# A two-layer decoder trunk on one core: the second layer's retention values as one seven-product block multiplication, its weight sums made during the first layer's MLP

## The chip, the cores and the metric

The kernel runs on one core of a Trainium2 chip. A core has a matrix engine (TensorE, PE in the profile; its weight loads have their own row, PEld), a vector engine (VectorE, DVE), a scalar engine (ScalarE, ACT), GpSimd (POOL), and SyncE (SP), which here issues nearly all DMAs, in order, from one queue. The metric is the device time of one execution in microseconds (us). A matmul multiplies a stationary block of 128x128 by a moving block 128 deep and up to 512 wide and adds into a bank of PSUM (128 partitions by 512 floats; there are eight banks).

## The reference: what is computed

There are 512 tokens, a model width of 1024, and two layers. Each layer:

```
h = rmsnorm(x, g_mix);  z = h @ w_in
aq, ak, av, rq, rk, rv, rg, ga, gb = split(z)
ya = sliding_window_attention(aq, ak, av, sinks) @ w_a
r  = chunkwise_retention(rq, rk, rv)        # 4 heads, keys 128 wide, values 256 wide
yb = (group_norm(r) * silu(rg)) @ w_b
x  = x + (sigmoid(ga) * ya + sigmoid(gb) * yb) @ w_out
x  = x + relu(rmsnorm(x, g_mlp) @ w_up)**2 @ w_down
```

The change concerns `rv`, the retention values: 512 tokens by 1024 features, a product of the 512x1024 input with a 1024x1024 part of `w_in`.

## The kernel before, in words

**Numbers.** Every factor is held as a high and a low part (`split`, L336: ScalarE copies to the high part in a rounded format, VectorE subtracts to get the low part), and each product is three matmuls: high by high, high by low, low by high (`products`, L326).

**Weights.** All weights come in units of 128x1024 floats (512 KB) in one fixed order (`unit_order`, L59). `unit` (L292) hands out the next one and keeps the following ones on their way: `load_until` (L186) issues the DMA on SP's queue into one of three "raw" buffers, `split_until` (L262) makes the high part on ScalarE (L286) and the low part on VectorE (L287) into one of three buffers each. A chunk of 128 output features (`chunk`, L375) takes one unit and 24 matmuls; a group of four chunks (`group`, L387) takes four units and 96.

**Products by seven.** For most of `w_b`, `w_out` and `w_up` a pair of units is multiplied as a 2x2 block matrix with seven block products in place of eight (`narrow_pair` L651, `wide_pair` L1347). They need sums of the weight blocks, and sums of the input blocks, "forms", which `sum_input` (L616) makes with four 128x512 VectorE operations and two 128x1024 splits. For five pairs per layer (`PARKED`, L54) the weight sums are made ahead: `raws_ahead` (L230) loads two units into two buffers of the "big" pool (seven buffers of 128x1024), `sums_ahead` (L237) does four 128x512 VectorE operations, behind the low part last issued, and writes four pieces of 256 KB to DRAM ("park"), from where `load_part` (L211) later loads them.

**The retention values.** `values` (L962) makes half of `rv` (two heads, 512 features) for all tokens: four units, for each of 8 input chunks and 4 token blocks three matmuls with the weights moving 512 wide, 96 in all, into four banks; then `split` with a scale per token (L342, L343).

**The order of a layer's first half** (L1129 to L1208): attention's projections; gates, `qk(0)` and four `rg` chunks, with attention running in the background; two sets of weight sums loaded; `drain`; `qk(1)`; `values(0)`; `w_a` (four units, 96 matmuls on the attention's output); in between, `ahead` at five places makes the weight sums and loads further sets; then `retention(0)` (heads 0 and 1) in the background of `qk(2)`, `qk(3)` and `values(1)`; `drain`; `retention(1)` in the background of four `rg` chunks and eight `gb` chunks; `drain`; then `w_b`.

**The background.** `retention` (L1095) is a generator; `advance` (L359) gives it a step each time that enough credit has come together. `chunk` calls `advance(rate)` before each half of its 24 matmuls, `values` once per input chunk. A retention needs 17 steps: scores (4), outputs of the two heads (the last one is step 10), their norms (the second is step 13), finish (15 and 16), and `sum_input` of its results (17). `drain` runs what is left with no matmuls of a chunk beside it.

**Who orders the instructions.** The order in which code is written is a priority. A scheduler with a timing simulation takes, engine by engine, what is ready in its simulated time, so an instruction can be issued earlier or later than its place in the code; each engine then runs its list in order. `tc.issue_after(ins)` holds instructions behind `ins` on its engine.

**The MLP** (L1448 on): the first group of `w_up`, then pairs of `w_up` in turn with two chunks of `w_down`, for four quarters q of the hidden layer. In the first layer the last quarter's `w_down` is one group and four chunks; each result is added to x, scaled, split, squared and summed, and x is stored to DRAM ("spill", L1440). Then the second layer begins with a group of `w_in`, in which the sum of squares goes through a matmul (L478).

## Time and profile before

| | |
|---|---|
| time, median of 3 runs | 1468.88 us (1468.85 to 1469.62) |
| span of the profiled execution, first to last instruction | 1467.5 us |
| PE busy | 1461.0 us, 7434 matmul records |
| PEld busy | 1246.4 us |
| DVE busy | 1161.6 us |
| ACT busy | 814.6 us |
| DMA | 198.65 MB, mean 135 GB/s |

The time of the profiled execution itself was not taken apart from its span; the median of the runs is 1.4 us more than the span, which lies before the first and behind the last instruction. In the timeline each row has the start in us, the duration in us, engine, line, operation, output<-inputs, shape and count; in the groups each row has a count, then total busy time in us, the mean of one in ns, and the engine's idle time before it. A matmul's duration there overlaps the next one's start, so the distance between starts is what it costs. A few matmul records are missing. In the tables by stretch each engine has its busy us and its count, then come the granted clock of the matrix engine (1.00 is full), the DMA engines' share and the GB/s.

### The profile page before, as it was taken

To read this page: it belongs to the slowest core of one execution; us is meant where nothing else is said; L and a number is where in the kernel's file an instruction comes from. 1 tells how busy PE (TensorE), PEld (TensorE's weight loads), DVE (VectorE), ACT (ScalarE), POOL (GpSimd) and SP (SyncE) were. 2 spreads that over 40 slices of the span, in tenths; PEclk is the share of its full clock that TensorE was granted. 3 is DMA by queue.
4 is the path that set the end of the run, shared out by engine and by line. 5 is a ranking of instruction groups with operands and counts; after the bars stand their busy time and mean duration, and the time that the engine had idled before them with its cause. 6 is when DMAs were issued, how large, how long until landed. Compare 5 with 4: busy or idle time off the path is not lost.

```text
span 1467.5 us, 20166 instructions
## 1 busy us (share of the span) xinstructions
PE 1461.0 (100%) x7434; PEld 1246.4 (85%) x7434; DVE 1161.6 (79%) x1912; ACT 814.6 (56%) x1306; POOL 3.7 (0%) x14
## 2 busy tenths in 40 slices
PE   9999999999999999999999999999999999999998
PEld 7888888888988888888888888888989888888887
DVE  7998778678988787776678977786899877877774
ACT  7657356654684445444456653666547754455544
POOL 0000000000000000000000000000000000000000
PEclk9999999999999999999999999999999999999999
DMA  6423843356443332333543258323654432333373
GB/s 227 134 87 101 280 166 98 104 171 210 130 120 125 101 115 88 107 108 115 165 121 102 86 168 285 107 95 107 191 197 123 144 101 87 125 105 101 108 200 108
DMA packets 73346, 198.65 MB, mean 135 GB/s; under 512 B 8712, under 2 KB 8864, under 8 KB 73248
## 3 DMA queue, kind: packets, MB, share of 16 engines
q1 hardware_dynamic: 72960, 196.84, 42.5%
q8 instruction: 58, 0.95, 0.3%
q10 hardware_dynamic: 288, 0.52, 0.1%
q14 instruction: 40, 0.33, 0.1%
HBM read 173.73 MB, written 20.98 MB: 133 GB/s over the span
## 4 chain that ended last, share of the span: by engine, by line
PE 99%; DVE 0%; issue 0%; POOLq 0%; ACT 0%; DVEq 0%; ACTq 0%
PE mm L334 24%; PE mm L332 23%; PE mm L333 23%; PE mm L1356 11%; PE mm L1357 6%; PE rv L332 2%; PE rv L334 2%; PE rv L333 2%; PE score L864 1%; PE r L332 1%; PE r L334 1%; PE r L333 1%; PE pT L819 0%; PE pv L846 0%; PE pv L845 0%; PE warm L311 0%
## 5 line engine op out<-in xcount | busy, mean ns | idle before, releaser
L333 PE MATMUL mm<-r,hi 128*128 128x512 f32 (+1 forms) x1568 | 572.5, 367 | 0.0
L332 PE MATMUL mm<-r,hi 128*128 128x512 f32 (+1 forms) x1568 | 569.9, 367 | 0.0
L334 PE MATMUL mm<-r,lo 128*128 128x512 f32 (+1 forms) x1568 | 563.9, 367 | 0.2
L286 ACT ACTIVATE hi<-raw 128x1024 fp32r<-128x1024 f32 (+1 forms) x334 | 333.9, 1002 | 377.8 <-PE mm L333 206.9
L287 DVE TENSOR_TENSOR lo<-raw,hi 128x512 fp32r<-128x512 f32 (+1 forms) x335 | 384.3, 1150 | 110.8 <-ACT hi L286 109.4
L334 PEld LDWEIGHTS mm<-r,lo 128*128 128x128 f32 x1568 | 293.6, 188 | 48.8 <-DVE lo L287 1.4
L332 PEld LDWEIGHTS mm<-r,hi 128*128 128x128 f32 x1568 | 294.1, 188 | 46.5 <-ACT r L342 0.2
L333 PEld LDWEIGHTS mm<-r,hi 128*128 128x128 f32 x1568 | 294.3, 188 | 46.0
L1356 PE MATMUL mm<-r,hi 128*128 128x512 f32 x728 | 252.0, 391 | 0.0
L1357 PE MATMUL mm<-r,lo 128*128 128x256 f32 x728 | 200.3, 277 | 0.0
L1356 PEld LDWEIGHTS mm<-r,hi 128*128 128x128 f32 x728 | 136.5, 188 | 28.7 <-ACT mm L1383 0.2
L1357 PEld LDWEIGHTS mm<-r,lo 128*128 128x128 f32 x728 | 136.7, 188 | 3.2 <-DVE lo L287 0.6
L1429 ACT ACTIVATE z<-z 128x512 f32<-128x512 f32 x56 | 32.5, 624 | 51.8 <-DVE z L1409 51.8
L1436 DVE TENSOR_TENSOR x<-x,mm 128x512 f32<-128x512 f32 x56 | 37.7, 686 | 28.1 <-PE mm L334 28.1
L334 PE MATMUL rv<-hi,r 128*128 128x512 f32 x128 | 49.8, 389 | 0.0
L333 PE MATMUL rv<-lo,r 128*128 128x512 f32 x128 | 49.8, 389 | 0.0
L332 PE MATMUL rv<-hi,r 128*128 128x512 f32 x128 | 49.8, 390 | 0.0
L339 ACT ACTIVATE r<-z 128x512 fp32r<-128x512 f32 x64 | 38.5, 619 | 16.3 <-DVE z L1090 16.1
L340 DVE TENSOR_TENSOR r<-z,r 128x512 fp32r<-128x512 f32 x64 | 42.9, 685 | 4.7 <-ACT r L339 4.3
L891 ACT ACTIVATE sm<-sm,st 128x256 f32<-128x256 f32 (+1 forms) x64 | 30.1, 472 | 19.0 <-DVE st L879 18.8
L1409 DVE SCALAR_TENSOR_TENSOR z<-z,rstd 128x512 f32<-128x512 f32 x52 | 35.6, 685 | 0.6
L340 DVE TENSOR_TENSOR r<-sums,r 128x1024 fp32r<-128x1024 f32 x24 | 28.9, 1216 | 0.0
(270 smaller groups left out, 1679.2 us busy)
## 6 DMA issues: line engine op xcount, KB each, us to landing
raw<-w_in_in SPq DMA_DIRECT2D x89, 512.0 KB, 3.6
raw<-w_down_in SPq DMA_DIRECT2D x64, 512.0 KB, 3.6
raw<-w_up_in SPq DMA_DIRECT2D x32, 512.0 KB, 3.9
raw<-w_up_in SPq DMA_DIRECT2D x60, 256.0 KB, 2.9
raw<-w_a_in SPq DMA_DIRECT2D x8, 512.0 KB, 6.5
ahead<-w_b_in SPq DMA_DIRECT2D x8, 512.0 KB, 5.4
park_w_b<-ahead SPq DMA_DIRECT2D x16, 256.0 KB, 5.9
ahead<-w_up_in SPq DMA_DIRECT2D x8, 512.0 KB, 5.7
```

The lines of the kernel that those rows point to most:

```text
L286: nc.scalar.activation(hi[:, at], raw[:, at], AF.Copy)
L287: last_low[:] = [nc.vector.tensor_tensor(lo[:, at], raw[:, at], f32(hi[:, at]), ALU.subtract).ins]
L332: nc.tensor.matmul(ps, ah, bh, start=start and i == 0, stop=False, **more)
L333: nc.tensor.matmul(ps, ah, bl, start=False, stop=False, **more)
L334: nc.tensor.matmul(ps, al, bh, start=False, stop=stop and i == n - 1, **more)
L339: nc.scalar.activation(hi, src, AF.Copy)
L340: nc.vector.tensor_tensor(lo, src, f32(hi), ALU.subtract)
L1356: nc.tensor.matmul(both, hi[:, c], m, start=start and k == 0, stop=False, **more)
L1357: nc.tensor.matmul(ps[:, :H], lo[:, c], m[:, 0, :], start=False, stop=k == 3 and start, **more)
L1409: nc.vector.scalar_tensor_tensor(z[:, :, at], z[:, :, at], 0.0, factor, ALU.max, ALU.mult)
L1429: nc.scalar.activation(z[:, i, :], z[:, i, :], AF.Square)
L1436: nc.vector.tensor_tensor(x[:, c, :], x[:, c, :], ps, ALU.add)
```

## The change

In the second layer, `values(0)` and `values(1)` give way to `all_values`, behind `w_a`: the whole `rv` as a 2x2 block product (halves of the 1024 inputs by halves of the 1024 features) with seven block products. A block product takes two units, and per unit 2 parts by 2 token blocks by 3 matmuls, all 512 wide, into two banks. Three of the seven weight blocks are plain units of `w_in`, four are sums loaded from "park". The forms of the input are made from x as it was stored in DRAM (`raw_forms`), around `qk(1)`. `retention(0)` starts behind `all_values`, at 1.25 steps per half chunk through `qk(2)` and `qk(3)`, and is not drained before `retention(1)`. The weight sums of the second layer, its five sets and four new ones for the values, are made in the first layer's MLP: three beside the `w_down` chunks of the first quarter, six in the last `w_down`.

```diff
+VALUES = (("w_in", 22), ("sum", 0), ("sum", 1), ("w_in", 24), ("sum", 2), ("sum", 3), ("w_in", 32))
...
+    if last:
+        order = plain("w_in", 22) + plain("w_a", 4)
+        order += [("value", block, u) for block in range(len(VALUES)) for u in range(2)]
+        order += plain("w_in", 26, 30) + plain("w_in", 34, 46)
...
+    AHEAD_VALUES = tuple(("w_in", k) for k in range(KD // 2))
...
+    def load_value(i):
+        layer, _, block, u = order[i]
+        name, n = VALUES[block]
+        raws[i] = raw_tile()
+        if name == "w_in":
+            nc.sync.dma_start(raws[i], w_in[layer, n + u])
+        else:
+            for j, side in enumerate((LEFT, RIGHT)):
+                nc.sync.dma_start(raws[i][:, side], park["w_in", 2 * u + j][:, n, :])
...
+    def load_ahead():
+        if to_load:
+            to_sum.append((*to_load[0][1:], raws_ahead(*to_load.pop(0))))
+
+    def sum_ahead():
+        if to_sum:
+            with tc.issue_after(last_low[0]):
+                sums_ahead(*to_sum.pop(0))
+
+    def ahead():
+        sum_ahead()
+        load_ahead()
...
+        def raw_forms(by_form, ks):
+            b = [big("xr") for _ in range(2)]
+            for part, g in ((0, ks), (1, ks + 4)):
+                nc.sync.dma_start(b[part], spill[:, g : g + 2, :])
+                for i in range(2):
+                    col = g_mix * KD + g + i
+                    nc.scalar.activation(b[part][:, i, :], b[part][:, i, :], AF.Copy, scale=gain[:, col : col + 1])
+            sum_input(by_form, b, ks)
+
+        def all_values(form):
+
+            a, (e, b) = [bank(ps_aux, "rv") for _ in range(2)], [[bank(p, "rv") for p in (q, ps_mm)] for q in (ps_aux, ps_mm)]
+            eu, bu = big("eu"), big("bu")
...
+            def multiply(two, moving, start):
+                for u in range(2):
+                    hi, lo = unit("value", layer)
+                    for i in range(2):
+                        k, cols = 2 * u + i, slice(i * T, (i + 1) * T)
+                        for j, ps in enumerate(two):
+                            m = moving[k][:, :, j * P : (j + 1) * P]
+                            pair = ((m[:, 0, :], m[:, 1, :]), (hi[:, cols], lo[:, cols]))
+                            products(ps, [pair], start and k == 0, k == 3, not start)
...
+            multiply(a, block(0, 0), True)
+            for j in range(2):
+                nc.scalar.activation(b[j], a[j], AF.Copy)
+            multiply(e, form(0), True)
+            for j in range(2):
+                nc.scalar.activation(eu[:, j, :], e[j], AF.Copy)
+            multiply(b, form(1), False)
+            for j in range(2):
+                nc.scalar.activation(bu[:, j, :], b[j], AF.Copy)
+            multiply(a, block(1, 0), False)
+            for j in range(2):
+                keep_values(0, j, a[j])
+            multiply(b, form(2), False)
+            add_up(1, b, eu)
+            multiply(e, block(1, 1), False)
+            add_up(0, e, bu)
+            multiply(b, form(3), False)
+            for j in range(2):
+                keep_values(1, j, b[j])
...
-        qk(1, between=ahead)
-        values(0, ahead)
+        if last_layer:
+            homes_v = [forms_home() for _ in range(4)]
+            by_form_v = [h[1] for h in homes_v]
+            raw_forms(by_form_v, 0)
+            qk(1)
+            raw_forms(by_form_v, 2)
+        else:
+            qk(1, between=ahead)
+            values(0, ahead)
...
-        background.append(retention(0))
-        qk(2)
-        qk(3)
-        values(1)
-        drain()
+        if last_layer:
+            all_values(form_of(by_form_v))
+            for t, _ in homes_v:
+                slots.give(*t[1])
+            background.append(retention(0))
+            qk(2, 1.25)
+            qk(3, 1.25)
+        else:
+            background.append(retention(0))
+            qk(2)
+            qk(3)
+            values(1)
+            drain()
...
+        if not last_layer:
+            to_load.extend((layer + 1, *at) for at in (*PARKED[2:], *PARKED[:2], *AHEAD_VALUES))
...
                 two_chunks("w_down", layer, up[q], [put_down(2 * i), put_down(2 * i + 1)], turning)
...
+                if not last_layer and q == 0:
+                    sum_ahead()
+                    if i < 3:
+                        load_ahead()
...
                 new_input()
-                all_of(group("w_down", layer, up[q], [put_down(c, True) for c in range(4)]))
+                load_ahead()
+                all_of(group("w_down", layer, up[q], [put_down(c, True) for c in range(4)], {0: ahead, 2: ahead}))
                 for c in range(4, KD):
                     chunk("w_down", layer, up[q], put_down(c, True))
+                    ahead()
```

More of the change, by code (lines that the diff above doesn't have):

```diff
@@ L163, in decoder @@
     spill, aside = (dram.tile([P, KD, T], F32, name=n) for n in ("spill", "aside"))
-    order = [(layer, *u) for layer in range(DEPTH) for u in unit_order()]
+    order = [(layer, *u) for layer in range(DEPTH) for u in unit_order(layer == DEPTH - 1)]
     raws, parts, homes = {}, {}, []
@@ L204, in decoder @@
     LEFT, RIGHT = slice(0, UNIT // 2), slice(UNIT // 2, UNIT)
-    park = {at: dram.tile([P, 4, T], F32, name="park_%s_%d" % at) for at in PARKED}
+    AHEAD_VALUES = tuple(("w_in", k) for k in range(KD // 2))
+    park = {at: dram.tile([P, 4, T], F32, name="park_%s_%d" % at) for at in PARKED + AHEAD_VALUES}
     def is_parked(i):
@@ L981, in values, with keep_values, add_up @@
                 rv[pair, b] = (hi, lo)
+        def raw_forms(by_form, ks):
[9 more added lines that the diff above has]
+            eu, bu = big("eu"), big("bu")
+            def keep_values(pair, n, src):
+                hi, lo = slots.one(), slots.one()
+                split(view(hi), view(lo), src, rcol[:, n : n + 1])
+                rv[pair, n] = (hi, lo)
+            def multiply(two, moving, start):
[7 more added lines that the diff above has]
+                            products(ps, [pair], start and k == 0, k == 3, not start)
+            def add_up(pair, two, kept):
+                for j in range(2):
+                    nc.vector.tensor_tensor(kept[:, j, :], two[j], kept[:, j, :], ALU.add)
+                    keep_values(pair, 2 + j, kept[:, j, :])
+            multiply(a, block(0, 0), True)
[15 more added lines that the diff above has]
+            multiply(b, form(3), False)
+            for j in range(2):
+                keep_values(1, j, b[j])
```

24 lines of the change are left out of this document (13 added, 11 removed).

## The prediction, made before the changed kernel was run

> **What bounds the kernel now.** I read the page first: busy times, the granted clock and the chain of work that ended last.
>
> ```profile
> span 1467.5 us, 20166 instructions
> PE 1461.0 (100%) x7434; PEld 1246.4 (85%) x7434; DVE 1161.6 (79%) x1912; ACT 814.6 (56%) x1306; POOL 3.7 (0%) x14
> PEclk9999999999999999999999999999999999999999
> PE 99%; DVE 0%; issue 0%; POOLq 0%; ACT 0%; DVEq 0%; ACTq 0%
> ```
>
> The matrix engine is the bound in every stage: it ends 99% of the chain, at full clock. So matmuls taken away count in full, and whatever makes PE wait counts in full too; work on VectorE (79%), ScalarE and the DMAs costs nothing until PE waits for it. The sum below is made against the span of 1467.5 us; the median, 1468.88, is 1.4 above it, and I add that back. A measurement of this kernel can tell about 0.2% from no change, 2.9 us.
>
> Next, what a retention-value matmul costs: its group on the page, then the first `values` of the second layer as one stretch (matmuls on the tile rv alone).
>
> ```profile
> L334 PE MATMUL rv<-hi,r 128*128 128x512 f32 x128 | 49.8, 389 | 0.0
> 871.70:893.49 21.79, 21.79 (x96) 1.00 0.86 277
> ```
>
> The 389 ns overlap with the next matmul. From the start of the first to the end of the stretch, 96 matmuls follow each other in 21.79 us, 0.227 each, with nothing between them. That is the price that counts. The Trainium skill ("TensorE: Matmul & The Clock Gate", Part 1) gives a warm 512-wide matmul 215.7 ns from start to start; by that the 24 matmuls below would be worth 5.2 us instead of 5.45. The stretch is this kernel's own, so I stay with it.
>
> **Part by part.**
>
> *The product.* Before, the two `values` of the second layer are 2 x 96 = 192 matmuls. After, seven block products of 2 units x 2 parts x 2 token blocks x 3 are 168, of the same shape. 24 x 0.227 = **-5.45 us**. Nothing else on PE is added: the seeding of banks and the joins are copies and adds elsewhere.
>
> *The feeding of the product.* Units go from 8 to 14, so a unit lasts 12 matmuls, 2.72 us, where it lasted 5.45.
>
> ```profile
> L287 DVE TENSOR_TENSOR lo<-raw,hi 128x1024 fp32r<-128x1024 f32 x291 | 354.7, 1220 | 105.0 <-ACT hi L286 103.5
> L286 ACT ACTIVATE hi<-raw 128x1024 fp32r<-128x1024 f32 x291 | 307.3, 1057 | 364.3 <-PE mm L333 204.6 <-PE mm L1356 101.3 <-issue 26.3
> L343 DVE SCALAR_TENSOR_TENSOR r<-rv,rcol,r 128x512 fp32r<-128x512 f32 x16 | 11.3, 749 | 4.1 <-ACT r L342 4.1
> L1169 DVE TENSOR_TENSOR x<-x,mm 128x512 f32<-128x512 f32 x16 | 10.9, 684 | 6.1 <-PE mm L334 6.0
> ```
>
> A unit takes 1.06 us of ScalarE and 1.22 of VectorE, one behind the other 2.28, less than 2.72, and three buffers are in turn; most high parts wait for PE to free a buffer (204.6 + 101.3 us idle), so the feed is ahead. 512 KB in 2.72 us is 193 GB/s, under the 277 of the stretch above. The copies between banks lie beside the next product, 5.45 us long. The tight seam is before the seventh product: behind the fifth, VectorE has two adds (0.684) and two splits (0.749) beside two low parts (1.22), 5.3 of 5.45 us, before the bank is free. I take **+0.2** (0 to 1.5).
>
> *The sums leave the second layer's mixer and the forms come in.* Five sets of four operations of 0.685 us, 13.7 of VectorE, go; `raw_forms` brings 8 of 0.68 and 4 splits of 1.2, 10.3. PE waited for neither. No gain.
>
> *`w_a` moves forward.* It now starts where `values(0)` did, at 871.70. It multiplies attention's output, whose last low part is this row:
>
> ```profile
> 871.84 0.68 DVE L340 TENSOR_TENSOR r<-whole,r 128x512 fp32r<-128x512 f32 x1
> L340 DVE TENSOR_TENSOR r<-sums,r 128x1024 fp32r<-128x1024 f32 x24 | 28.9, 1216 | 0.0
> L339 ACT ACTIVATE r<-sums 128x1024 fp32r<-128x1024 f32 x24 | 24.9, 1053 | 3.0 <-DVE sums L627 1.6 <-DVE sums L630 1.5
> L639 ACT ACTIVATE xg<-x 128x512 f32<-128x512 f32 x16 | 10.4, 710 | 0.0
> ```
>
> It is ready at 872.52, where 21.8 us of `values(0)` used to cover it. `w_a`'s second matmul would need it at 871.93: 0.6 us of waiting in place of none. The first `raw_forms` runs just ahead, 4 x 0.710 + 2 x 1.053 = 4.9 us on ScalarE and 4 x 0.68 + 2 x 1.216 = 5.2 on VectorE; queued in front of that split it would delay it by 5. It comes later in the code than the split, so I take **+0.6** (0 to 5).
>
> *Six sets of sums in the first layer's last `w_down`*, from about 690 to the second layer's first sum of squares at 744.6. Stretches, then the rows of that boundary:
>
> ```profile
> 690.00:744.00 54.00, 54.00 (x242) 44.77 (x241) 31.84 (x41) 23.07 (x33) 0.00 (x0) 1.00 0.50 160
> 711.00:744.00 33.00, 33.00 (x147) 27.31 (x147) 23.27 (x31) 16.59 (x24) 0.00 (x0) 1.00 0.52 170
> 871.00:915.00 44.00, 44.00 (x198) 36.57 (x197) 33.06 (x47) 14.13 (x18) 0.00 (x0) 1.00 0.86 277
> L241 DVE TENSOR_TENSOR ahead<-ahead 128x512 f32<-128x512 f32 x10 | 6.8, 685 | 0.0
> 739.18 0.69 DVE L340 TENSOR_TENSOR sh<-rest,sh 64x512 fp32r<-64x512 f32 x1 [0.70 <-ACT sh L339]
> 744.60 0.39 PE L478 MATMUL ssq<-sh,ones 128*128 128x512 f32 x1
> 708.62 0.33 SPq L196 DMA_DIRECT2D raw<-w_in_in  x1
> 733.50 0.39 PE L332 MATMUL mm<-r,hi 128*128 128x512 f32 x1
> ```
>
> VectorE has 33 - 23.3 = 9.7 us free from 711 to 744, where four sets need 4 x 4 x 0.685 = 11.0. The sum of squares has 744.60 - 739.87 = 4.7 us to spare, so 1.3 us of overflow are covered. New weights are loaded 733.50 - 708.62 = 25 us ahead; each `ahead` load stands in SP's queue in front of them and may wait for park writes, for which those 25 us are the cover. The first three sets lie in the first quarter at one per 20 us. I take **+0.3** (0 to 7, worked out under the second rival).
>
> *Retention starts later and is not drained in between.* A half chunk is 12 matmuls, 2.72 us. Before, the last outputs of `retention(1)` (step 10) come at half chunk 8 of the `rg` chunks, so 17 half chunks are still to run before `w_b`: 17 x 2.72 + 1.9 of its own matmuls = 48 us. The trace has them here:
>
> ```profile
> 1009.57 0.39 PE L332 MATMUL r<-r,r 128*128 128x512 f32 x1
> 1022.85 0.69 DVE L340 TENSOR_TENSOR sh<-rest,sh 64x512 fp32r<-64x512 f32 x1
> 1027.04 0.39 PE L478 MATMUL ssq<-sh,ones 128*128 128x512 f32 x1
> 1043.34 1.22 DVE L340 TENSOR_TENSOR r<-sums,r 128x1024 fp32r<-128x1024 f32 x1
> 1046.71 0.28 PE L332 MATMUL mm<-r,hi 128*128 128x256 f32 x1
> 971.00:995.00 24.00, 24.00 (x115) 20.25 (x114) 21.30 (x38) 13.68 (x22) 0.00 (x0) 1.00 0.35 110
> ```
>
> `w_b` starts at 1046.71, 37.1 us after the outputs, so they lagged by 11. The chain from them to the last form of `w_b`'s input ends at 1044.56: 35.0 us, of which 1027.04 - 1023.54 = 3.5 is the norm's matmul waiting for its place on PE, so 31.5 is work and queueing. After the change step 10 of `retention(1)` is step 26 in all; at 1.25 per half chunk it falls to half chunk 21 of 32, and 12 x 2.72 + 1.9 = 34.6 us remain. Without a lag this covers 31.5: no wait. With the whole lag of 11, 23.5 are left against up to 35.0: 11.5 us of waiting. The lag came with a crowded VectorE (21.3 of 24 us in the stretch that holds the splits of `values(1)` and the drained end of `retention(0)`). The splits now lie earlier, but `qk(2)` and `qk(3)` take steps faster. I take **+1.0** (0 to 11.5), near the end without lag, because PE has waited at none of these places so far.
>
> Sum: -5.45 + 0.2 + 0.6 + 0.3 + 1.0 = -3.35. Span 1464.15, time **1465.5 us**.
>
> **Rivals.**
>
> *Retention's tail takes PE (slower).* Place: the end of the `gb` chunks, before the first `w_b` pair; the products there need `retention(1)`, and its forms 12 narrow matmuls later. For it: the 2.2 us (1046.71 - 1044.56) that were left before, and 14 us less time behind step 10. Against it: the order is a scheduler's, and the lag's cause partly moves. At 8 to 11.5 us with the other terms at 1.1: 1468.9 - 5.45 + 1.1 + 8 to 11.5 = 1472.5 to 1476. It ends slower from 7.3 us of waiting on. Chance 0.15. At part of that price, 2.5 to 7 us, the time is 1467 to 1471.5, no change: chance 0.18.
>
> *The sets come late at the layer boundary (no change).* Each set reads 1 MB and writes 1 MB. The stretch from 690 to 744 moves 54 x 160 = 8.6 MB; six sets add 12.6, in all 21.2. At share 0.86 the second layer's sums moved 277 GB/s, so 322 at a full share, and 21.2 MB take 66 us: 12 us late. Less the 4.7 to spare, VectorE, which takes its list in order, would hold the sum of squares by 7.3 us. The Trainium skill ("DMA: Bandwidth & Descriptors", Specifications) puts the ceiling at 435 GB/s; by that it would be 49 us, in time, and this rival would be nothing. No row here reaches 435. Against it in the rows: in the mixer VectorE never sat idle before a set's first operation (0.0 in its group's row), since the sums were placed late enough. At half the price 1468.9 - 5.45 + 1.8 + 3.6 = 1468.9. Chance 0.15.
>
> *The busy price.* If a matmul's 389 ns were its cost, 24 would give 9.3 us: 1468.9 - 9.3 + 2.1 = 1461.7. The 21.79 us for 96 speak against it. The Trainium skill ("Perfetto Trace Analysis", Identifying the Most-Contended Engine) likewise calls matmul busy time a poor measure, as matmuls are pipelined. Chance 0.02. That the change doesn't take its 24 matmuls away is not open: both counts stand in the code.
>
> **How the numbers follow.** My own forecast, 1462.5 to 1465.9, has 0.50; with the busy price, faster has 0.52. No change, from the partial tail and the late sets, has 0.33. Slower, the full tail, has 0.15. The forecast lies close to the bound of 1465.9, since small waits would eat the rest. The range goes from 1462.5, with only 1 us of waiting, to 1472.0, where the partial tail and the late sets end; above it lies most of the full tail.
>
> **What would show it.** Right: rv matmuls 168 in the second layer in place of 192, at 0.227, with no PE gap inside; `w_a`'s first matmuls less than 1 us apart from `qk(1)`; `w_b`'s first narrow matmul within 2 us of the last `gb` matmul; the sum of squares of the second layer at about 745. Wrong: a PE gap of several us before `w_b` that ends on a VectorE or ScalarE form or on retention's split (the tail); VectorE idle on an `ahead` load near 730 to 745 and the sum of squares late (the sets); a gap before `w_a` that ends on attention's split; or gaps inside the seven products that end on a low part.

## The result and the profile after

The changed kernel takes 1481.53 us (median of 4 runs, 1481.1 to 1482.15), the kernel before 1468.87 on the same chip: ratio 1.0085, 95% interval 1.0071 to 1.01. It is 12.7 us slower, where 3.4 us faster was forecast. The span of its profiled execution is 1479.2 us, 11.7 longer.

The page of the kernel after, the four lines that were read first before:

```profile
span 1479.2 us, 20294 instructions
PE 1461.5 (99%) x7410; PEld 1244.8 (84%) x7410; DVE 1187.6 (80%) x1950; ACT 831.4 (56%) x1330; POOL 3.7 (0%) x14
PEclk9999999999999999999999999999899999999999
PE 95%; DVE 2%; ACT 1%; issue 1%; DMA 0%; POOLq 0%; DVEq 0%; ACTq 0%
```

24 matmul records fewer, and yet 0.5 us more of PE time: some matmuls ran slowly, and PEclk has an 8 in one slice. VectorE, ScalarE and "issue" now hold 4% of the chain. The stretch of the product (tile rv alone, then all tiles) and PE's waits (total us, times, longest) say where the loss is not, and what PE waited for:

```profile
897.85:937.84 39.99, 38.86 (x168) 31.19 (x167) 3.99 (x6) 5.42 (x9) 1.00 0.57 177
897.85:937.84 39.99, 39.99 (x181) 33.20 (x179) 27.27 (x33) 23.85 (x31) 0.00 (x0) 1.00 0.57 177
PE mm L357 <- ACT r L364: 6.9, 3, 4.1
PE mm L358 <- DVE r L365: 2.6, 2, 1.7
PE mm L357 <- DVE z L1087: 1.0, 1, 1.0
```

The product does what it should: 168 matmuls and nothing idle between them. The other 13 in its stretch are scores of the first retention: the scheduler starts them at 925.05, inside the product, though the code has them behind it. The waits sit at two places. Ahead of `w_a`, at 867 to 876 us, there are 1.0 us (z, at 868.87, before the second chunk of `qk(1)`) and 1.3 of the 6.9 (at 875.94, before `w_a` itself). The rest, 5.6 + 2.6 = 8.2 us, is behind the start of `w_b`. Rows of that tail on PE, then VectorE's list from the last norm to the last form:

```profile
985.83 0.39 PE L357 MATMUL ret<-r 128*128 128x512 f32 x1
1029.49 0.39 PE L357 MATMUL r<-r,r 128*128 128x512 f32 x1
1045.83 0.39 PE L503 MATMUL ssq<-sh,ones 128*128 128x512 f32 x1
1046.06 0.28 PE L357 MATMUL mm<-r,hi 128*128 128x256 f32 x1
1048.04 3.35 DVE L505 RECIPROCAL inv<-inv 128x512 f32<-128x512 f32 x1
1051.42 1.29 DVE L1184 TENSOR_TENSOR z<-z,inv 128x512 f32<-128x512 f32 x2
1055.76 2.48 DVE L966 TENSOR_TENSOR gb<-mm,rstd 128x512 f32<-128x512 f32 x4
1060.82 1.22 DVE L365 TENSOR_TENSOR r<-sums,r 128x1024 fp32r<-128x1024 f32 x1
```

The first row is the first score of `retention(1)`, the second its last output (1009.57 before), the third the fourth head's norm (1027.04 before), the fourth the first product of `w_b` (1046.71 before), the last the last form (1043.34 before). `w_b` starts 0.65 us earlier than before; its last form is done at 1062.04, 17.5 us later. Before, the forms were 2.2 us ahead of `w_b`; now they are 16.0 behind.

The stretch from the second pair's first score to the last form, before and after:

```profile
969.58:1044.56 74.98, 74.98 (x351) 63.02 (x350) 58.37 (x89) 47.67 (x68) 0.00 (x0) 1.00 0.33 103
```
```profile
985.83:1062.04 76.21, 68.07 (x328) 57.55 (x327) 58.50 (x88) 44.65 (x69) 0.00 (x0) 0.95 0.37 118
```

It is nearly as long as before, 76.2 us against 75.0, and VectorE is busy for the same 58 us of it. What changed is its start: the first score comes 16.2 us later, and `w_b` does not. Stretches of the place where `w_b` waits, in the kernel after:

```profile
1045.00:1050.00 5.00, 4.88 (x36) 4.42 (x34) 3.10 (x2) 2.00 (x3) 0.00 (x0) 1.00 0.50 132
1050.00:1055.00 5.00, 0.38 (x1) 0.19 (x1) 4.93 (x7) 1.56 (x3) 0.00 (x0) 0.96 0.30 87
1055.00:1060.00 5.00, 2.23 (x7) 1.64 (x7) 5.00 (x9) 4.73 (x7) 0.00 (x0) 0.50 0.50 178
1060.00:1065.00 5.00, 4.37 (x20) 4.31 (x21) 3.36 (x5) 2.76 (x5) 0.00 (x0) 0.52 0.44 155
```

PE runs out of products that need no forms at 1049.6 and stands; VectorE is busy 9.93 of the 10 us from 1050 to 1060. And when PE goes on, its granted clock is 0.50 to 0.52 for some ten us, so the 2.23 + 4.37 us of matmuls there cost about twice what they should: some 3.3 us on top of the 8.2. The Trainium skill ("TensorE: Matmul & The Clock Gate", Part 1) says that the clock falls to half after an idle window of about 3.4 us; here 4.1 us of waiting came before it.

The third place does not show as a long wait. The stretch of the first quarter in the first layer's MLP, before, after, and in two of the runs below (the five sets alone; the sets moved away):

```profile
440.00:560.00 120.00, 120.00 (x606) 101.77 (x605) 94.81 (x145) 59.10 (x89) 0.00 (x0) 1.00 0.34 109
```
```profile
440.00:560.00 120.00, 119.29 (x596) 100.19 (x595) 98.76 (x156) 57.57 (x88) 0.00 (x0) 1.00 0.48 162
```
```profile
440.00:560.00 120.00, 117.96 (x587) 98.74 (x586) 97.45 (x153) 56.00 (x85) 0.00 (x0) 1.00 0.48 161
```
```profile
440.00:560.00 120.00, 120.00 (x605) 101.72 (x604) 94.61 (x147) 59.55 (x91) 0.00 (x0) 1.00 0.35 111
```

In the same 120 us PE starts 10 matmuls fewer, at 120 / 606 each 2.0 us. The size varies: in the third row, with the same three sets, it is 19 fewer, 3.8 us. The sum of the places against the span: -5.45 (product) + 2.0 (first quarter) + 2.3 (`w_a`) + 8.2 + 3.3 (tail) = +10.4, of 11.7 measured; the other 1.3 are not traced to a place.

### The profile page after: what moved, and what is told of

The parts are those of the page before. It is cut to its first block, busy times and chain, and to the rows that moved or that the text cites. A ratio compares the mean times of both kernels' runs of the same rounds, so it can differ in the third digit from the quotient of the medians.

```text
span 1479.2 us, 20294 instructions
## 1 busy us (share of the span) xinstructions
PE 1461.5 (99%) x7410; PEld 1244.8 (84%) x7410; DVE 1187.6 (80%) x1950; ACT 831.4 (56%) x1330; POOL 3.7 (0%) x14
## 4 chain that ended last, share of the span: by engine, by line
PE 95%; DVE 2%; ACT 1%; issue 1%; DMA 0%; POOLq 0%; DVEq 0%; ACTq 0%
PE mm L357 23%; PE mm L358 23%; PE mm L359 23%; PE mm L1454 11%; PE mm L1455 5%; PE rv L358 2%; PE rv L357 2%; PE rv L359 2%; PE score L905 1%; PE r L357 1%; PE r L359 1%; PE r L358 1%; ACT hi L311 1%; DVE lo L312 0%; PE pT L860 0%
## 5 line engine op out<-in xcount | busy, mean ns | idle before, releaser
L311 ACT ACTIVATE hi<-raw 128x1024 fp32r<-128x1024 f32 (+1 forms) x340 | 340.2, 1003 | 368.2 <-PE mm L358 184.9
L312 DVE TENSOR_TENSOR lo<-raw,hi 128x512 fp32r<-128x512 f32 (+1 forms) x341 | 392.2, 1153 | 102.3 <-ACT hi L311 100.6
L358 PE MATMUL rv<-lo,r 128*128 128x512 f32 x120 | 46.8, 390 | 0.0
L359 PE MATMUL rv<-hi,r 128*128 128x512 f32 x120 | 46.7, 390 | 0.0
L357 PE MATMUL rv<-hi,r 128*128 128x512 f32 x120 | 45.1, 390 | 0.0
L365 DVE TENSOR_TENSOR r<-sums,r 128x1024 fp32r<-128x1024 f32 x28 | 33.8, 1219 | 0.0
```

Source lines behind the costliest of these rows:

```text
L311: nc.scalar.activation(hi[:, at], raw[:, at], AF.Copy)
L312: last_low[:] = [nc.vector.tensor_tensor(lo[:, at], raw[:, at], f32(hi[:, at]), ALU.subtract).ins]
L357: nc.tensor.matmul(ps, ah, bh, start=start and i == 0, stop=False, **more)
L358: nc.tensor.matmul(ps, ah, bl, start=False, stop=False, **more)
L359: nc.tensor.matmul(ps, al, bh, start=False, stop=stop and i == n - 1, **more)
L365: nc.vector.tensor_tensor(lo, src, f32(hi), ALU.subtract)
```

## The experiments

Theory one: the second retention's end, now behind the whole product, takes PE ahead of `w_b`, because it starts too late and is paced too thinly. Rivals: the weight sums in the first layer's MLP are what costs; `w_a`'s place is; or VectorE's line, not start or pace, sets the tail. Names below are those of the runs; "after" is the changed kernel. All ratios are against the kernel before, which took 1468.87 to 1469.76 us beside the runs; differences between runs of about 1 us say nothing.

**The sets alone, and the chain alone.** `e1_sets_only` takes the product back and leaves five sets in the first layer's MLP (`seven` is False, at both places of the mixer):

```diff
-    order = [(layer, *u) for layer in range(DEPTH) for u in unit_order(layer == DEPTH - 1)]
+    order = [(layer, *u) for layer in range(DEPTH) for u in unit_order(False)]
...
-        if last_layer:
+        if seven:
...
-            to_load.extend((layer + 1, *at) for at in (*PARKED[2:], *PARKED[:2], *AHEAD_VALUES))
+            to_load.extend((layer + 1, *at) for at in (*PARKED[2:], *PARKED[:2]))
```

> The block product of seven is left out: the second layer's mixer is the kernel before's, with plain value products, but its five sets of sums are still made in the first layer's MLP (the six sets of the seven product are not made). Theory one (the tail of the second retention, behind the seven product, costs about 12 us): only the first quarter's 2 us stay, so about 1470.5 us, at most 1473, and no stall of TensorE ahead of w_b. Theory two (the sums moved into the first layer's MLP are what costs): most of the 12.7 us stay, 1477 to 1481 us.

1471.34 us, ratio 1.0015 (1.0006 to 1.0023), 2.1 us slower than before, with no wait ahead of `w_b`. As theory one had it: the sets cost 2 us and not 12.

`e7_no_last_norm` is after without the fourth head's norm:

```diff
             def norm(self):
+                if last_layer and self.h == 3:
+                    return
...
-                    nc.vector.tensor_tensor(z, z, self.inv, ALU.mult)
+                    if not (last_layer and h == 3):
+                        nc.vector.tensor_tensor(z, z, self.inv, ALU.mult)
```

> The kernel after without the norm of the fourth head in the second layer: its sum of squares, its inverse root and its two multiplications by it are left out (13 small instructions of the computation). If the chain behind the last outputs (sum of squares, ssq at 1045.83 us, reciprocal until 1051.4, multiplications) is what w_b waits for: the forms are ready some 10 us earlier, no wait ahead of w_b and no halved clock, 1469 to 1471 us. If the outputs themselves or VectorE's load are late: the wait shrinks by the 5 us of left-out work at most, 1476 us or more.

1470.69 us, ratio 1.0009 (0.9999 to 1.0018): 10.8 us below after. The last form, and the stretch that held the stall:

```profile
1048.88 1.22 DVE L365 TENSOR_TENSOR r<-sums,r 128x1024 fp32r<-128x1024 f32 x1
1050.00:1055.00 5.00, 4.67 (x40) 4.46 (x39) 2.78 (x5) 2.18 (x5) 0.00 (x0) 1.00 0.73 209
```

The form is ready at 1050.10 where it was 1062.04, PE is busy 4.67 of the 5 us where it had 0.38, and the clock stays at 1.00. Together the two runs show where the bulk is lost: `w_b` waits for the end of the fourth head, and with its norm left out the rest of the change costs what the product saves, plus 1.4 us. What they leave open is why that end comes 16 us late. Nor do they tell the norm's waiting from its work, since the edit takes both away.

**The pace.** `e2_rate_1_7` and `e8_no_empty_steps`:

```diff
-            qk(2, 1.25)
-            qk(3, 1.25)
+            qk(2, 1.7)
+            qk(3, 1.7)
...
-            chunk("w_in", layer, xs, put_rg(i), 1.25)
+            chunk("w_in", layer, xs, put_rg(i), 1.7 if last_layer else 1.25)
```

> The kernel after with 1.7 steps of the retention in each half chunk of qk(2), qk(3) and of the last four rg chunks, where it has 1.25. Theory one (the retention starts too late and is paced too thinly): its last outputs come about 5.7 half chunks (some 18 us) earlier, the wait ahead of w_b goes and the clock stays up there: 1468 to 1472 us. Rival (VectorE and ScalarE, not the pace, set the retention's end): the steps only queue behind the engines, TensorE stalls inside qk(2) and the rg chunks instead, 1479 to 1484 us.

```diff
+            if last_layer and pair == 1:
+                for head in two:
+                    for e in range(2):
+                        head.outputs(e)
+                        yield
+                two[0].norm()
+                yield
+                two[1].norm()
+                yield
+            else:
...
```

> The kernel after with the second retention's six empty steps taken out, so that its four outputs follow each other and the two norms follow them. In steps the last outputs come 2 earlier and the end 5 earlier than in the kernel after. Theory one (pace): the last norm starts some 4 to 8 us earlier, 1474 to 1478 us. Rival (the engines' own order and latency set it, as the run with 1.7 steps suggests, which did not gain): 1481 us, within 1.5.

1482.25 (1.0074 to 1.0104) and 1479.53 us (1.005 to 1.0084): pace is not it. Without the empty steps the last output comes 8 us earlier (1021.43) and the fourth head's norm 9 (1036.87), and yet the last form only 2.3 (1059.77): what lies between them got longer. With 1.7 steps PE also waits 1.16 and 0.97 us for VectorE in the `rg` chunks, as the rival had it. The second pair's first score comes 4.5 us earlier, and its last form 2:

```profile
981.30 0.39 PE L357 MATMUL ret<-r 128*128 128x512 f32 x1
990.97 0.69 DVE L1184 TENSOR_TENSOR z<-z,inv 128x512 f32<-128x512 f32 x1 [3.97 <-DMA inv<-row]
1057.64 2.44 DVE L365 TENSOR_TENSOR r<-sums,r 128x1024 fp32r<-128x1024 f32 x2
```

The middle row is a place where an ordered list costs time. The first pair's last multiplications wait 3.97 us for their norm's DMA, and VectorE's work on the second pair's scores stands behind them. It does not explain the run by itself, since after has the same wait, 3.64 us at 997.04. From first score to last form it is 78.8 us (1060.08 - 981.30); after has 76.2, the kernel before 75.0.

**The start.** `e6_scores_early` puts the first pair's four score steps into the product's fifth and sixth blocks; `e11_one_run` adds a single generator for both retentions, in which the second pair's scores stand ahead of the first pair's last steps, at 1.7 (the new `True` makes `multiply` call `advance` once per unit):

```diff
+            background.append(retention(0))
-            multiply(b, form(2), False)
+            multiply(b, form(2), False, True)
             add_up(1, b, eu)
-            multiply(e, block(1, 1), False)
+            multiply(e, block(1, 1), False, True)
```

> The kernel after with the four score steps of the first retention put inside the block product of seven, where VectorE is free (in its fifth and sixth blocks, their banks from the other pool), so that the retention has 30 steps left behind it where it had 34. Theory one: the second retention comes 3.2 half chunks (9 to 10 us) earlier and most of the wait ahead of w_b goes, 1470 to 1474 us. Rival (the end is set by VectorE and ScalarE in the rg and gate chunks): 1480 to 1483 us.

```diff
+            yield from scores(heads[:2])
+            yield from outputs(heads[:2])
+            yield from scores(heads[2:3])
+            yield from scores(heads[3:])
+            yield from finish(0)
+            yield from outputs(heads[2:])
+            yield from finish(1)
```

> The kernel after with both retentions of the second layer as one run of steps: the first two heads' scores inside the block product of seven, their four outputs and two norms without empty steps, then the third and the fourth head's scores as soon as qk(2) and qk(3) are through, and only then the first pair's last steps; 1.7 steps in each half chunk. From the first score of the second pair to the last form the kernel before took 75.0 us and the kernel after 76.2, so theory one (the tail's cause is when that chain starts, not how fast it is paced): it starts at about 970 us instead of 985.8, ends at about 1046, and the wait goes: 1469 to 1473 us. Rival (the same work closer together fills VectorE, and the chain grows as it did with 1.7 steps, to 78.8 us): 1476 to 1480 us.

1479.45 (1.0054 to 1.0082) and 1480.31 us (1.006 to 1.0087). The first pair's scores did start earlier, at 909.59 and 908.32 where after has 925.05, but the second pair's first score moved by only 4 us, to 981.90 and 981.76, and the last form by 2.2 and 2.4. So neither run tests an early start of the second pair. Rows of the second run: the fourth head's norm 11.9 us earlier than in after, then VectorE.

```profile
1033.96 0.39 PE L503 MATMUL ssq<-sh,ones 128*128 128x512 f32 x1
1038.81 0.69 DVE L1189 TENSOR_TENSOR z<-z,inv 128x512 f32<-128x512 f32 x1 [4.78 <-DMA inv<-row]
1045.00:1060.00 15.00, 11.18 (x43) 9.27 (x44) 14.48 (x23) 8.94 (x14) 0.00 (x0) 0.66 0.47 158
1057.30 2.36 DVE L365 TENSOR_TENSOR r<-sums,r 128x1024 fp32r<-128x1024 f32 x2 [0.32 <-ACT r L364]
```

The chain stands 4.78 us behind a DMA, and then VectorE is busy 14.48 of 15 us with multiplications, sums, forms, low parts and the gate chunks' evacuations, until 1059.66, where after has 1062.04. In this run PE's longest wait there, 3.70 us at 1045.09, is for the low part of a weight, which VectorE makes too. So the rival gained ground: the tail is VectorE's list.

**`w_a`.** `e3_forms_late` moves `raw_forms(by_form_v, 0)` behind `qk(1)` in the program; `e10_behind_attention` binds the raw forms and the silu on ScalarE behind the split of the attention's last block (`last_part` is its high part on ScalarE):

```diff
-            raw_forms(by_form_v, 0)
             qk(1)
+            raw_forms(by_form_v, 0)
             raw_forms(by_form_v, 2)
```

> The kernel after with the first half of the raw forms made behind qk(1) instead of ahead of it, so that ScalarE's four scalings and the sums stand behind the rotations of qk(1). If TensorE's 2.5 us of stalls ahead of w_a come from that work standing ahead of them: 1479 to 1480 us. If w_a's place alone makes them: no change, 1481.5 us. If the forms now come late for the first products that use them: 1483 us or more.

```diff
-            raw_forms(by_form_v, 0)
             qk(1)
-            raw_forms(by_form_v, 2)
+            with tc.issue_after(last_part[0]):
+                raw_forms(by_form_v, 0)
+                raw_forms(by_form_v, 2)
+                for i in range(4):
+                    silu(i)
```

> The kernel after with ScalarE's four scalings of the raw forms and its silu of four rg chunks bound behind the split of the attention's last block (an edge on ScalarE, where the earlier run had only another place in the program and ScalarE's order stayed the same). If TensorE's stall of 1.7 us and 0.8 ahead of w_a is that ScalarE work standing ahead of the split: it goes, 1479 to 1480 us, and if nothing else moves the rest stays as after. If the forms then come late for the product's second block: the gain is lost in the product, 1481 to 1484 us.

The first: 1481.35 us, no change. It did not test what it was meant to, since ScalarE's list came out the same; here after, then this run, with silu and scalings ahead of the split in both:

```profile
874.05 1.32 ACT L1030 ACTIVATE xr<-xr,x 128x512 f32<-128x512 f32 x2
875.27 0.61 ACT L364 ACTIVATE r<-whole 128x512 fp32r<-128x512 f32 x1
```
```profile
873.46 1.32 ACT L1030 ACTIVATE xr<-xr,x 128x512 f32<-128x512 f32 x2
874.68 0.61 ACT L364 ACTIVATE r<-whole 128x512 fp32r<-128x512 f32 x1
```

The second: 1479.24 us, ratio 1.0069 (1.0056 to 1.0082), 2.3 us below after; the 1.3 us wait is gone from PE's list, the 1.0 us one stays. So the 1.3 us came from ScalarE's order, which the place in the program does not set. `e12_both` has this edit and the single run of steps:

> Both edits of the two other runs in one kernel. If the tail and the stall ahead of w_a are separate costs, the gains add: 1467 to 1471 us, about the kernel before, with the first quarter's 2 us still there. If the forms bound behind the attention delay the product, the sum of the gains is not reached: 1472 us or more.

1478.9 us (1.0052 to 1.0077): 2.6 below after, hardly more than the edge alone. The tail stayed, so the forecast of 1467 to 1471 missed.

**More cover.** `e5_w_a_behind` moves `w_a` behind the product, under the first retention, with a step at each of its chunks, and has the product take its two plain blocks first:

```diff
             all_values(form_of(by_form_v))
             background.append(retention(0))
+            attention_out()
             qk(2, 1.25)
             qk(3, 1.25)
```

> The kernel after with w_a moved behind the block product of seven, in front of qk(2), and the first retention begun with it (a step at each of its eight chunks); the product takes its two plain blocks first, so that its forms may come later. The same matmuls; 21.8 us of TensorE work (96 matmuls of 0.227 us) that nobody waits for now lies inside the retentions' cover instead of ahead of it. Theory one (what the tail costs is cover that the change took from the retentions: the plain second product used to lie between them): the wait ahead of w_b goes, and the stall ahead of w_a with it, 1466 to 1470 us. Rival (the second retention's own chain behind qk(3) is too long, whatever lies ahead of it): the tail stays, 1478 us or more. A new stall at the product's first form would show at its third block, up to 5 us.

1481.34 us (1.0069 to 1.0099), no gain, for two reasons in its rows: the product now begins 32 us earlier, before its operands are ready, and PE waits 5.2 us in it, with the granted clock at 0.94 over its stretch; and the second pair's first score still came at 984.16, behind `qk(2)` and `qk(3)`. `e13_qk_ahead` takes both ahead of `w_a`, has the early scores, and runs both retentions as one list of steps (the minus line of the next diff):

```diff
-        order = plain("w_in", 22) + plain("w_a", 4)
+        order = plain("w_in", 22) + plain("w_in", 26, 30) + plain("w_a", 4)
...
+            qk(1)
             raw_forms(by_form_v, 0)
-            qk(1)
+            qk(2)
             raw_forms(by_form_v, 2)
+            qk(3)
...
-            qk(2, 1.25)
-            qk(3, 1.25)
```

> The kernel after with qk(2) and qk(3) ahead of w_a instead of behind the product, the first pair's scores inside the product, and both retentions as one run of steps at 1.25 that begins the second pair's scores right behind the first pair's outputs. The same matmuls in another order; behind the product only the four rg and eight gate chunks are left as cover, 65 us, but no rotations are left in VectorE's line there. Theory one (the second pair's start is held by qk(2) and qk(3), whose rotations end at 964 to 982 us): its first score comes at about 955 to 965 us, the last form at about 1035, no wait ahead of w_b, and the stall ahead of w_a goes since four chunks lie behind the attention: 1465.5 to 1469 us. Rival (VectorE's work in the retentions is what takes the time): with less cover behind the product the tail stays or grows, 1478 us or more.

1476.24 us (1.0031 to 1.0059), 5.3 below after; 1.3 of that is the wait ahead of `w_a`, gone here too. It lies between the two expectations. In the next diff o is a head's two outputs, a and b the first and the second of them, n its norm, f its finish, + a pair's sums and y an empty step. `e16_order` and `e15_order_1_7` change the order of the second pair's steps, then the pace too:

```diff
-("o", 2), ("f", 0), ("a", 3), ("n", 2), ("f", 1), ("b", 3), ("+", 0), ("y", 0), ("n", 3), ("f", 2), ("f", 3), ("+", 1)
+("o", 2), ("f", 0), ("f", 1), ("o", 3), ("n", 2), ("n", 3), ("+", 0), ("f", 2), ("f", 3), ("+", 1)
```

> The run with qk(2) and qk(3) ahead of w_a, with the steps of the second pair in another order at the same pace of 1.25: the fourth head's two outputs stand right behind each other, ahead of both norms, and the first pair's sums behind the norms. If the order in VectorE's line is what stretches the chain behind the last output: the last form comes at 1046 to 1050 us, 1469 to 1472 us. If not: 1475 to 1477 us as before it.

> The same order with 1.7 steps in each half chunk of the rg and gate chunks. Theory (behind the product only pace and order are left to set the tail, since no rotations are in the line): the last outputs come at about 1000 us, the last form ahead of w_b, no wait and no halved clock there: 1466 to 1469 us, the first run not slower than the kernel before. Rival (VectorE's work of some 65 to 70 us between the product and the last form cannot be packed closer): 1474 us or more.

1475.59 (1.0027 to 1.0055) and 1476.94 us (1.0041 to 1.0069): neither order nor pace. With the other order the fourth head's norm comes 10 us earlier than in `e13_qk_ahead` (1026.10 against 1036.13), and the last form 0.5 later: VectorE is busy 38.8 of the 45.0 us between the last output and it. With the pace too, PE waits 3.88 us for a weight's low part instead. What was left to try was taking work out of the tail. `e17_outputs_inside` reorders the product's blocks, so that the first pair's values are done after the fifth, and runs the first pair's scores in blocks two and three and three of its four output steps in blocks six and seven (the last argument of `multiply` names the units that begin with a step); `e18_outputs_inside_1_5` has 1.5 steps in the `rg` chunks:

```diff
-            multiply(e, form(0), True)
+            background.append(retentions())
+            multiply(e, form(0), True, (0, 1))
...
-            multiply(b, form(1), False)
+            multiply(b, form(1), False, (0, 1))
...
-            multiply(b, form(2), False, True)
-            multiply(e, block(1, 1), False, True)
+            multiply(e, block(1, 1), False)
+            add_up(0, e, bu)
+            multiply(b, form(2), False, (1,))
+            multiply(b, form(3), False, (0, 1))
```

> The run with qk(2) and qk(3) ahead of w_a and the other order, with the product's blocks ordered so that the first pair's values are done after the fifth block, and with the first pair's scores in its second and third block and three of its four output steps in its sixth and seventh: behind the product the second pair's scores come at once. Theory (the retentions' VectorE work has to lie under the product): the second pair's first score comes at 960 to 965 us, its last output at about 1000, the last form at or before the first narrow matmul: 1466 to 1469.5 us. Rival (the chain behind the last output and the gate chunks' evacuations fill VectorE however early it starts): 1473 us or more.

> The same with 1.5 steps in each half chunk of the four rg chunks. If pace still matters once the work is spread: 1 to 2 us below the run with 1.25. If VectorE's line is what counts: the same, or up to 1 us above.

1471.09 us (ratio 1.0016, 1.0007 to 1.0025) and 1472.0 us (1.0009 to 1.0026). The first gives back 10.4 of the 12.7 us; it is 1.6 above its forecast's upper end, and pace again buys nothing. Its rows: last output, norm, last form, and VectorE's stretches between.

```profile
1006.03 0.47 PE L357 MATMUL r<-r,r 128*128 128x512 f32 x1
1020.58 0.50 PE L503 MATMUL ssq<-sh,ones 128*128 128x512 f32 x1 [0.24 <-DVE sh L365]
1020.00:1030.00 10.00, 9.76 (x43) 7.79 (x42) 9.51 (x10) 3.77 (x5) 0.00 (x0) 1.00 0.34 102
1030.00:1040.00 10.00, 10.00 (x45) 8.27 (x45) 10.00 (x15) 6.63 (x8) 0.00 (x0) 1.00 0.35 100
1040.00:1050.00 10.00, 8.21 (x50) 7.20 (x49) 10.00 (x14) 7.28 (x12) 0.00 (x0) 1.00 0.73 236
1050.32 1.23 DVE L365 TENSOR_TENSOR r<-sums,r 128x1024 fp32r<-128x1024 f32 x1
```

The fourth head's norm is now 25 us earlier than in after, the last form 10.5: between them VectorE is busy 29.5 of 30 us. `e19_sums_earlier` moves the first pair's sums out of that stretch, between the fourth head's two outputs:

> The run with the first pair's outputs inside the product at 1.25 steps, with the third head's norm and the first pair's sums put between the fourth head's two outputs instead of behind them. If VectorE's line behind the last output is what is left of the tail: 3 to 5 us less of it, the last form about 1047 us, no idle time ahead of the second narrow pair: 1468.5 to 1470 us, no slower than the kernel before by more than 0.1%. If the sums only delay the fourth head's norm: 1471 to 1473 us.

1472.77 us (1.0014 to 1.0034), no gain: behind the sums the fourth head's second output came 7 us later, its norm at 1031.43, and the last form 1.5 us later.

Three runs side by side (us), with the stretch from the product's end to the last form of each below:

| run | product's end | last form | between | VectorE busy of it | `w_b` starts | form late by | median us |
|---|---|---|---|---|---|---|---|
| after | 937.84 | 1062.04 | 124.2 | 92.5 | 1046.06 | 16.0 | 1481.53 |
| e13 | 960.3 | 1056.63 | 96.3 | 73.3 | 1043.95 | 12.7 | 1476.24 |
| e17 | 962.6 | 1051.55 | 89.0 | 72.4 | 1044.56 | 7.0 | 1471.09 |

```profile
937.84:1062.04 124.20, 116.06 (x554) 98.06 (x553) 92.54 (x145) 74.93 (x117) 0.00 (x0) 0.97 0.34 109
```
```profile
960.30:1056.63 96.33, 90.45 (x441) 76.43 (x440) 73.30 (x115) 63.04 (x95) 0.00 (x0) 0.99 0.35 111
```
```profile
962.60:1051.55 88.95, 86.83 (x419) 73.16 (x418) 72.39 (x111) 57.96 (x90) 0.00 (x0) 0.99 0.37 114
```

VectorE is busy 75 to 81% of that time in each; the rest is waits in its ordered list, in after 9.1 us for the norms' DMAs, 8.3 for high parts of weights and most of the others for ScalarE too. In these three the time follows how late the form is, and the form follows how much retention work is left behind the product's end. The second pair's first score is at 985.83, 976.51 and 970.96 us in them. From it to the last form it takes 76.2, 80.1 and 80.6 us, and 74.1 to 82.3 in the other runs of the product that keep the norm: an earlier start comes through in part, and nothing made that chain much shorter.

**The sets.** `e4_sets_spread` makes the first quarter's three sets one per quarter; `e14_sets_in_mixer` is `e13_qk_ahead` with the three made in the first layer's mixer. There the two layers' parked sums share their places in DRAM, so the first layer multiplies three pairs with the second layer's sums; the work is of the same size.

```diff
-                if not last_layer and q == 0:
-                    sum_ahead()
-                    if i < 3:
-                        load_ahead()
+                if not last_layer and i == 0:
+                    load_ahead()
+                if not last_layer and i == 2:
+                    sum_ahead()
```

> The kernel after with the three sets of sums that are made in the first quarter of the first layer's MLP spread over its first three quarters, one in each, loaded at the quarter's first step and summed at its third. If the first quarter's cost comes from three sets in a row (loads ahead of the weights' own, sums ahead of the evacuations): 1479.7 to 1480.5 us. If each set costs the same wherever it stands: 1481.5 us. If later quarters have less room: 1482.5 us or more.

> The run with qk(2) and qk(3) ahead of w_a, with the three sets of the first quarter of the first layer's MLP made in the first layer's mixer instead (one with w_a, one with rg chunks 4 and 5, one with gate chunks 2 and 3). If the first quarter's cost is its own full ScalarE and VectorE lines: 1.5 to 2 us below that run. If a set costs about 0.7 us wherever it is made: the same as that run. If the first retention's tail has no room either: 2 us or more above it.

1484.82 us (1.0088 to 1.0118), 3.3 above after, as if later quarters have less room. And 1476.18 us (1.0031 to 1.0057), the same as `e13_qk_ahead`: the first quarter is then clean (the fourth of the rows above, 605 matmuls), but the gain is lost in the mixer: by 372 us, ahead of the first layer's MLP, this run is 1.7 us behind the kernel before, where `e13_qk_ahead` is 0.3. No free place was found for the sets.

No version beat the kernel before. The nearest that keeps the product and computes everything is `e17_outputs_inside`.

## Why the prediction was wrong, point by point

- **The product, -5.45, and its feeding, +0.2: right.** 168 matmuls at 0.227, no gap inside, so the feeding cost nothing.
- **`w_a`, +0.6: mis-sized, 2.3.** 1.3 of it is the wait that was meant; the other 1.0, inside `qk(1)`, is a wait that the prediction does not have. Both together lie in the bounds (0 to 5), but the reason for taking the low end, that the raw forms come later in the code than the split, was wrong: ScalarE's list had silu and scalings first, whatever the place in the code; an edge took the 1.3 us away.
- **The sets, +0.3: 2.0, and elsewhere.** All of it is in the first quarter, which the prediction passes over with "one per 20 us". At the layer boundary the second rival's mechanism came as described, and cost nothing:

```profile
740.05 0.69 DVE L266 TENSOR_TENSOR ahead<-ahead 128x512 f32<-128x512 f32 x1 [4.00 <-DMA ahead<-w_in_in]
752.03 0.39 PE L503 MATMUL ssq<-sh,ones 128*128 128x512 f32 x1
720.00:760.00 40.00, 40.00 (x179) 33.10 (x178) 35.10 (x46) 18.16 (x25) 0.00 (x0) 1.00 1.00 361
```

  VectorE waited 4.00 us for a load, the DMAs were at share 1.00, and the sum of squares came 7.4 us late (7.3 were worked out, but some 2 of the 7.4 were brought along from the first quarter); still PE was busy 40.00 of 40, since other matmuls stood ahead of it. A late operation costs only what its next reader waits.
- **The retention's tail, +1.0: the step that failed, 11.5.** "I take +1.0 (0 to 11.5), near the end without lag, because PE has waited at none of these places so far." The chain behind the last output was right (32.6 us measured, 31.5 to 35 taken). The lag was not: the last output came 16.6 us ahead of `w_b` instead of 34.6, a lag of 18, where the kernel before has 11. "PE has waited at none of these places so far" was no evidence. Before, the second pair's first score came at 969.58, as the second value product ended, with 77.1 us to go to `w_b`, and its chain took 75.0; after, 60.2 were left for 76.2. A margin of 2 us says nothing about a change that takes 17 us of cover away.
- **The first rival, chance 0.15, is what happened.** Its place and its sign were right. Its price (8 to 11.5) met the measured 11.5 partly by luck: it took a lag of 11 where there were 18, the forms came 16.0 us late, products that need no forms covered some 3.7 of that, and 3.3 of the 11.5 are the lowered clock, which it did not have. Its time of 1472.5 to 1476 was too low, as it left the other terms at 1.1 (4.3 measured, with the first quarter and `w_a`), and 1.3 us are not traced. The range ended below it.

Why the lag is 18 was tested and is partly open. Shown: changing the pace or the order of steps does not remove the tail, nor does an earlier place for the first pair's scores alone; taking rotations, scores and outputs out from behind the product shortens it. Argued from the rows, not shown by itself: that VectorE's ordered list with its waits is what binds. A run that takes only those waits away was not made.

## What to carry to other kernels

When a change fuses two products into one, ask what was running under the first: the fused one delivers everything at its end, and all that consumed the first half early now lies behind it. Price that work by the engine that does it, with its in-order list, from the product's end to its next reader, and do not take the side of the bounds on which nothing has been late so far. An engine at 75 to 80% busy over a stretch may still be the bound when it takes its list in order and some entries wait for other engines and for DMAs; here that is argued, not shown.

## What the hardware showed that was not expected

The clock after a stall did not follow the length of one gap. In `e17_outputs_inside` a wait of 1.79 us was followed by a stretch at 0.66; in `e19_sums_earlier` PE waited 3.10 us, and the clock stayed at 1.00:

```profile
1048.74 0.38 PE L358 MATMUL mm<-r,hi 128*128 128x256 f32 x1 [1.79 <-DVE r L365]
1050.00:1055.00 5.00, 5.00 (x32) 5.00 (x31) 2.58 (x4) 2.19 (x4) 0.00 (x0) 0.66 0.77 239
```
```profile
1045.00:1050.00 5.00, 2.09 (x18) 1.89 (x17) 5.00 (x7) 4.97 (x7) 0.00 (x0) 1.00 0.51 182
1050.20 0.38 PE L357 MATMUL mm<-r,hi 128*128 128x256 f32 x1 [3.10 <-ACT mm L703]
1050.00:1055.00 5.00, 4.47 (x35) 4.26 (x36) 4.10 (x6) 2.52 (x5) 0.00 (x0) 1.00 0.80 236
```

The window of 3.4 us that the Trainium skill gives ("TensorE: Matmul & The Clock Gate", Part 1) does not explain the first of the two, which had no wait as long. The DMAs moved 361 GB/s over 40 us at share 1.00, where 322 had been worked out from a stretch at share 0.86.
